# Stick-breaking attention in units of 512 queries, with the gain of its norm applied where the transposed result is evicted

## The chip, the core and the metric

The kernel runs on one core of a Trainium2 chip. The metric is the device time of the whole program in microseconds: the median of several executions. One execution is also profiled; its rows are read below. The core has a matmul engine (PE, with its weight loads shown apart as PEld), a vector engine (DVE), a scalar engine for activations (ACT), GpSimd (POOL) and SyncE (SP), which here issues all transfers.

## What is computed

One decoder layer over 2048 positions and width 1024, in float32. Only the part that the change touches is shown: stick-breaking attention of 8 heads of 64, then an RMS norm over the 64 values of a head with the gain `sb_norm`.

```python
def one_block(args):
    q_blk, t0 = args
    rel = (t0 + jnp.arange(Q_BLOCK))[:, None] - k_pos[None, :]
    strict = rel > 0
    z = jnp.einsum('bhqd,bhkd->bhqk', q_blk, k) * scale
    log_beta = jax.nn.log_sigmoid(z)
    log_1mb = jnp.where(strict, jax.nn.log_sigmoid(-z), 0.0)
    between = lax.cumsum(log_1mb, axis=3, reverse=True) - log_1mb
    a = jnp.where(strict, jnp.exp(log_beta + between), 0.0)
    return jnp.einsum('bhqk,bhkd->bhqd', a, v)
...
sb_o = _rmsnorm(_stick_breaking_attention(sq, sk, sv), sb_norm[l])
mix = jnp.concatenate([diff_o, sb_o], axis=-1) @ w_o[l]
x = x + _rmsnorm(mix, attn_post_norm[l])
```

Before it stand a norm of the input and one q/k/v projection; beside it 4 heads of differential attention with 128 values; after it the output projection and a conv-gated FFN.

## The kernel before

The program is written as a stream of operations for a planner. `op` (L165) records an operation with its engine, an estimated duration, what it depends on and the buffers it uses; `Plan.run` (L180) then simulates the engines with these estimates and fixes the order of the instructions on each engine: of the operations that are ready, and whose buffers are free, the one that was recorded earliest in the planner's own time (`plan.now`) goes first. `copy` (L464) and `split` (L455) can go to either of two engines. So the estimates (`c_mm`, `c_act`, `c_scan`, L43 to L67) shape the order, and the hardware then runs each engine's list in order with semaphores. Buffers are tags with a count (`T`, L337): three PSUM banks "z" for scores, two "t" for transposes, one "o" for results, two "g" for projections; two each of `thi` and `tlo`; one each of `ot`, `os`, `sq`, `mix`, `mo`; and two rings, "w" of 8192 and "a" of 4096 columns, which are taken and given back in order of making.

Precision comes from splitting float32 values into a high and a low part (`hi`, `lo`), so most products are made of two or three matmuls.

Work is staged as follows. Heads come in 8 groups g: 0 to 3 are one differential head each, 4 to 7 are two stick-breaking heads m each. A projection pass p makes q, k and v of some groups for a range of 256-position tiles, and stores them to DRAM. `merge` (L928) interleaves the steps of heads and of projection passes in proportion to their estimated cost, so that the PE has projection matmuls among the attention's. At the end (L1379 to L1389) the last passes are merged with the last heads, the steps up to the mark (7, 5) run alone, and the remaining heads are merged with the first 8 blocks of the output projection (`wo_block`, L1086). `ffn_all` (L1178) follows.

In `sb_stream` (L954) a unit is (n, m, c): n stands for a group g and 256 queries s, m for a head, c for 512 keys, from the diagonal chunk down to 0. `front` (L959) makes, for each of two blocks jj of 128 queries, the scores z (L702, and L705 adds the mask on a diagonal), two sigmoids on ACT (L969 into a row `gm` of ring "a", L971 into a row `be` of ring "w"), a reversed running product on DVE (`scan`, L977), which starts from the last value of the chunk before (its row stays live as the carry), and a product on POOL (L982). A memset on POOL (L967) sets the last column of `gm`. Two units later `tstep` (L1012) transposes two key blocks by two query blocks into one "t" bank (`transp`, L712; L720), evicts it as `thi` (ACT or DVE, L466 and L467) and `tlo` (DVE, L734), and the step after multiplies with v (L1000): 256 queries wide, once with `thi` and once with `tlo`. On a diagonal the evictions are in two pieces, 256 and 128 wide.

`fin_sb` (L793) ends (g, s) for both heads together: copy the result out of "o" (L466), transpose (L799), add the two halves of v (L804, DVE), square (L806, POOL), sum (L807, DVE), mean and power -1/2 (L382 DVE, L384 POOL), then four scalar_tensor_tensor of 64 columns that multiply by the norm and by `sbn`, the gain broadcast to all partitions (L816, DVE). `mix_out` (L758) transposes the 256 columns back (L763), copies them out of PSUM (L466 or L467) and stores them to DRAM. `prefetch` (L746) loads q one s ahead and k, v one chunk ahead.

## Time and profile before

| | |
|---|---|
| median of the runs (3) | 3089.27 us |
| lowest and highest | 3088.21 and 3093.78 us |
| the profiled execution | 3094.23 us, of which the span 3092.5 us |
| mean granted clock of the PE | 0.992 |
| PE busy | 2984.5 us (97%), 17352 matmuls |
| DVE busy | 2252.0 us (73%) |
| ACT busy | 1442.9 us (47%) |
| POOL busy | 951.6 us (31%) |
| chain that ended last | PE 48% of the span, nearly all in the FFN (L1226 30%, L1311 16%) |

The profile is of one execution. A busy time is the time in which an engine had at least one instruction under way; matmuls overlap, so a busy PE isn't a PE at its peak. Times in the rows are in us from the start of the span, durations of one instruction in ns. An "idle before" is the time that the engine stood idle ahead of the instructions of a group, with what released it. Names of tiles stand without their numbers; ring_w and ring_a are the rings.

### The profile page before, as it was taken

Reading aid. Unit: us, or ns where it says so; the run is one execution under the profiler, and the core shown is the slowest. Engines: PE = TensorE matmul, PEld = TensorE weight load, DVE = VectorE, ACT = ScalarE, POOL = GpSimd, SP = SyncE. Lnnn points to the kernel's source line nnn. Section 1 sums busy time; section 2 is a strip of 40 time slices with the busy share of each in tenths; the row PEclk is TensorE's granted clock in tenths of the full one; section 3 lists DMA queues with packets and bytes.
Section 4 is the critical chain, followed back from the end, with each engine's and each line's share of the span. In section 5 each row is a group of like instructions: output and inputs, shape, how many; then the busy total and the mean of one; then the engine's idle time right before and its main releaser. Section 6 shows DMA issues by size and latency. Waiting matters only on the chain. (4 is left out here: it accounts for less than half of the span.)

```text
span 3092.5 us, 48117 instructions
## 1 busy us (share of the span) xinstructions
PE 2984.5 (97%) x17352; PEld 2610.4 (84%) x17352; DVE 2252.0 (73%) x4327; ACT 1442.9 (47%) x2913; POOL 951.6 (31%) x1047
## 2 busy tenths in 40 slices
PE   7999999999999999889999999999999999999998
PEld 7899999999888888868877888888888888888887
DVE  4658878897999999998754864387744776277742
ACT  4434545555777767666643433233322433233321
POOL 1001002002766777675411211033301332023310
PEclk9999999999999999999999999999999999999999
DMA  8776656655634366533363333443344333343332
GB/s 264 246 209 186 185 151 201 171 156 159 188 122 130 95 194 185 151 100 112 110 214 126 102 100 116 121 134 96 96 129 143 96 99 106 119 141 101 96 123 82
DMA packets 392146, 437.11 MB, mean 141 GB/s; under 512 B 20096, under 2 KB 328164, under 8 KB 381668
## 3 DMA queue, kind: packets, MB, share of 16 engines
q1 hardware_dynamic: 391908, 434.05, 46.7%
q8 instruction: 136, 2.23, 0.3%
q14 instruction: 102, 0.84, 0.1%
HBM read 333.30 MB, written 100.67 MB: 140 GB/s over the span
## 5 line engine op out<-in xcount | busy, mean ns | idle before, releaser
L1226 PE MATMUL pu<-fh,fhi 128*128 128x512 f32 x2816 | 869.0, 390 | 0.2 <-ACT fu L1234 0.2
L1226 PEld LDWEIGHTS pu<-fh,fhi 128*128 128x128 f32 x2816 | 529.4, 188 | 110.5 <-ACT fu L1234 0.6
L461 DVE TENSOR_TENSOR flo<-fraw,fhi 128x1024 fp32r<-128x1024 f32 x186 | 233.0, 1254 | 488.6 <-ACT fhi L458 488.5
L1226 PE MATMUL pu<-fh,flo 128*128 128x512 f32 x1408 | 549.2, 390 | 0.0
L982 POOL TENSOR_TENSOR ring_w<-ring_w,ring_a 128x512 f32<-128x512 f32 (+2 forms) x320 | 387.9, 1224 | 220.3 <-DVE ring_a L977 121.1
L605 PE MATMUL g<-hT,big 128*128 128x256 f32 x3072 | 447.8, 288 | 7.3 <-DVE st L638 4.3
L458 ACT CAST fhi<-fraw 128x1024 fp32r<-128x1024 f32 x253 | 265.5, 1051 | 397.4 <-PE py L1311 218.6
L1311 PE MATMUL py<-fhi,gt 128*128 128x512 f32 x1408 | 435.9, 390 | 0.0
L605 PEld LDWEIGHTS g<-hT,big 128*128 128x128 f32 x3072 | 405.4, 192 | 19.8 <-DVE st L638 4.4
L977 DVE TENSOR_TENSOR_SCAN ring_a<-ring_a 128x513 f32<-128x513 f32 (+2 forms) x320 | 412.8, 1316 | 6.1 <-ACT ring_a L969 6.1
L702 PE MATMUL z<-k,q 128*128 128x512 f32 (+3 forms) x1280 | 362.5, 376 | 10.4 <-ACT ring_a L969 7.0
L466 ACT CAST thi<-t 128x512 fp32r<-128x512 f32 (+2 forms) x472 | 221.6, 492 | 210.1 <-PE t L720 179.3
L1311 PEld LDWEIGHTS py<-fhi,gt 128*128 128x128 f32 x1408 | 264.5, 188 | 60.0
L1226 PEld LDWEIGHTS pu<-fh,flo 128*128 128x128 f32 x1408 | 264.7, 188 | 54.9
L734 DVE TENSOR_TENSOR tlo<-t,thi 128x512 fp32r<-128x512 f32 (+2 forms) x528 | 281.6, 556 | 34.6 <-ACT thi L466 28.4
L459 POOL TENSOR_TENSOR flo<-fraw,fhi 128x1024 fp32r<-128x1024 f32 x78 | 195.8, 2510 | 338.9 <-DVE fhi L457 171.2
L1311 PE MATMUL py<-flo,gt 128*128 128x512 f32 x704 | 277.8, 395 | 0.0
L720 PE MATMUL t<-ident,ring_w 128*128 128x128 f32 x1632 | 253.2, 276 | 22.4 <-DVE tlo L734 18.5
L1250 POOL TENSOR_TENSOR gt<-fy,gt 128x512 fp32r<-128x512 f32 x88 | 118.4, 1347 | 493.9 <-ACT gt L1249 483.0
L1239 DVE SCALAR_TENSOR_TENSOR fy<-fu,cw,fy 128x512 f32<-128x512 f32 x176 | 239.6, 1361 | 6.2
L384 POOL TENSOR_TENSOR sm<-sm,neghalf 128x2 f32<-128x2 f32 (+1 forms) x72 | 76.8, 1067 | 536.5 <-DVE sm L382 534.7
L602 PE MATMUL g<-big,hT 128*128 128x256 f32 x1536 | 227.4, 288 | 6.3 <-DVE st L624 1.5
(158 smaller groups left out, 4697.4 us busy)
## 6 DMA issues: line engine op xcount, KB each, us to landing
fraw<-in_w_up_dram SPq DMA_DIRECT2D x176, 512.0 KB, 3.8
hT<-hd SPq DMA_DIRECT2D x64, 1024.0 KB, 7.0
fraw<-in_w_down_dram SPq DMA_DIRECT2D x88, 512.0 KB, 3.8
q<-qd SPq DMA_DIRECT2D x128, 256.0 KB, 4.3
hd<-hT SPq DMA_DIRECT2D x16, 1024.0 KB, 5.4
qd<-st SPq DMA_DIRECT2D x128, 128.0 KB, 2.6
kd<-st SPq DMA_DIRECT2D x128, 128.0 KB, 2.6
vd<-st SPq DMA_DIRECT2D x64, 256.0 KB, 5.2
```

The source lines that it names most:

```text
L458: "ACT", c_act(n) + 42, lambda: nc.scalar.copy(hi(), raw()))
L461: "DVE", c_dvs(n), lambda: nc.vector.tensor_tensor(lo(), raw(), f32(hi()), ALU.subtract))
L602: nc.tensor.matmul(ps.t[:, cs], hk[:, b, c * P:(c + 1) * P], wv[:, a, k, :], start=first, stop=last)
L605: nc.tensor.matmul(ps.t[:, cs], wv[:, a, k, c * P:(c + 1) * P], hk[:, b, :], start=first, stop=last)
L702: nc.tensor.matmul(ps.t[:, 0:w], q.t[:, m, l, jj * P:(jj + 1) * P], kt.t[:, m, 0:w], start=(l == 0), stop=(l == 1 and not masked))
L720: nc.tensor.transpose(ps.t[:, cc * P:(cc + 1) * P], rows[jj].t[:, (k + kk) * P:(k + kk + 1) * P], ident)
L734: ol = op("DVE", c_dvp(n), lambda sl=sl: nc.vector.tensor_tensor(lo.t[:, sl], ps.t[:, sl], f32(hi.t[:, sl]), ALU.subtract), (oh,), (ps, hi ...
L977: nc.vector.tensor_tensor_scan(gr, gr, gr, 1.0 if cb is None else cb[0].t[:, 0:1], ALU.mult, ALU.bypass)
L982: rdeps.append(op("POOL", c_pool(w), lambda be=be, gm=gm, w=w: nc.gpsimd.tensor_tensor(be.t, be.t, gm.t[:, 1:w + 1], ALU.mult), (o1, o2), ...
L1226: nc.tensor.matmul(ps.t, w3(w)[:, k, :], h.t[:, a, k, :], start=(k == 0 and i == 0), stop=(k == KD - 1 and i == 2))
L1239: nc.vector.scalar_tensor_tensor(y.t, u.t[:, 1:TT + 1], cw[:, 1, f:f + 1], y.t, ALU.mult, ALU.add)
L1311: nc.tensor.matmul(ps.t, gt.t[:, a, j * P:(j + 1) * P], wt.t[:, ms], start=(m == 0 and i == 0), stop=(m == NFT - 1 and i == 2))
```

## The change

Stick-breaking units become (t, g, m, c) with t a tile of 512 queries: four blocks jj in a front, and the transposes follow one unit later, one key block by up to four query blocks in a "t" bank, evicted as one contiguous piece and multiplied with v 512 queries wide. Scores claim the two rows, and transposes claim `thi` and `tlo`, when they are planned. Each head m of 512 queries has its own end (`fin`): the square is made on ACT, the norm is applied to 256 columns in one DVE tensor_tensor with the norms broadcast, and when both heads are done, 512 columns are transposed and evicted by an ACT activation whose scale is `sbn`, now one gain per partition, and stored by two transfers. q is loaded per (t, g, m). The tile `sq` is gone, `mix` and `mo` have 512 columns, `sm` has 20 buffers; in `fin_diff` the square's output goes to spare columns of `ot`. The estimate of a matmul is proportional to its columns. The run up to (7, 5) is gone and the last merges have marks in the new units; (7, 2) is the same place in the work as (7, 4) was. Long stretches of removed lines are cut.

```diff
--- before.py
+++ after.py
@@ -41,7 +41,7 @@
 def c_mm(n):
-    return n / 2.4 + 2 if n > 128 else 80
+    return n * 0.4434
 
@@ -298,7 +298,7 @@
     subln = const.tile([P, P], F32, name="subln")
-    sbn = const.tile([P, 64], F32, name="sbn")
+    sbn = const.tile([P, 1], F32, name="sbn")
     cw = const.tile([P, 4, 2 * NFT], F32, name="cw")
@@ -335,13 +335,13 @@
     for name, n in (("hT", 4), ("big", 3), ("raw", 2), ("st", 2), ("k", 5), ("v", 5), ("q", 2),
-                    ("thi", 2), ("tlo", 2), ("mo", 1), ("ot", 1), ("os", 1), ("sq", 1), ("mix", 1),
+                    ("thi", 2), ("tlo", 2), ("mo", 1), ("ot", 1), ("os", 1), ("mix", 1),
                     ):
...
     T["t"] = Tag(2, fifo=False, bank=True)
-    T["sm"] = Tag(24, fifo=False)
+    T["sm"] = Tag(20, fifo=False)
     T["w"] = Ring(8 * 1024)
@@ -361,9 +361,9 @@
     sp = pool(left, "sp", "left")
-    fill_tags(sp, {"thi": ([P, 512], F32R), "tlo": ([P, 512], F32R), "mo": ([P, 256], F32),
-                   "ot": ([P, 512], F32), "os": ([P, 256], F32), "sq": ([P, 256], F32),
-                   "mix": ([P, 256], F32), "sm": ([P, 8], F32)})
+    fill_tags(sp, {"thi": ([P, 512], F32R), "tlo": ([P, 512], F32R), "mo": ([P, 512], F32),
+                   "ot": ([P, 512], F32), "os": ([P, 256], F32),
+                   "mix": ([P, 512], F32), "sm": ([P, 8], F32)})
     pp = pool(left, "pp", "left", PSUM)
@@ -444,7 +444,8 @@
                           (o,))
-        mem["sbn"] = load(lambda: sbn, sb_norm[0:1, :].to_broadcast([P, 64]), 32768)
+        mem["sbn"] = [load(lambda m=m: sbn[m * 64:(m + 1) * 64], sb_norm.rearrange("o p -> p o"), 256)
+                      for m in range(2)]
 
@@ -747,6 +748,8 @@
             load_q(*seq[n + 1])
+        else:
+            mem["sb_first"]()
         if s % 2 == 0:
@@ -762,11 +765,11 @@
         o = op("PE", 214, tr, deps, (ps, mx), what="mixT")
-        o = copy(lambda: mo.t, lambda: ps.t[:, 0:256], 256, (o,), (ps, mo))
-        mixs[g, s] = op(SPE, 0, lambda: nc.sync.dma_start(mixd[s][:, g, :], mo.t), (o,), (mo,), 0, 1 << 17, "mstore")
+        o = copy(lambda: mo.t[:, 0:256], lambda: ps.t[:, 0:256], 256, (o,), (ps, mo))
+        mixs[g, s] = op(SPE, 0, lambda: nc.sync.dma_start(mixd[s][:, g, :], mo.t[:, 0:256]), (o,), (mo,), 0, 1 << 17, "mstore")
 
     def fin_diff(g, s, po, last, rinv, rdeps):
-        ot, pq, os_, ss, junk, cm, mx = buf("ot"), buf("t"), buf("os"), small(), buf("sq"), small(), buf("mix")
+        ot, pq, os_, ss, cm, mx = buf("ot"), buf("t"), buf("os"), small(), small(), buf("mix")
         o = copy(lambda: ot.t[:, 0:256], lambda: po.t[:, 0:256], 256, (last,), (po, ot))
@@ -777,9 +780,9 @@
             for jj in range(2):
-                nc.scalar.activation(junk.t[:, 0:P], os_.t[:, jj * P:(jj + 1) * P], AF.Square,
+                nc.scalar.activation(ot.t[:, 256:384], os_.t[:, jj * P:(jj + 1) * P], AF.Square,
                                      scale=rinv.t[:, jj:jj + 1], accum_out=ss.t[:, jj:jj + 1])
-        o = op("ACT", 780, sq, (oc, *rdeps), (os_, junk, rinv, ss))
+        o = op("ACT", 780, sq, (oc, *rdeps), (os_, ot, rinv, ss))
         r, o = rs_ops(lambda: ss.t[:, 0:2], P, 2, (o,), (ss,))
@@ -788,34 +791,6 @@
         o = op("DVE", 71 + 2 * 263 + 127, fin, (o, mem["subln"]), (r, rinv, cm, os_, mx))
-        mix_out(g, s, mx, (o,))
...
         mix_out(g, s, mx, (o,))
@@ -951,86 +926,151 @@
 
-    def sb_stream(seq, begin, lag):
...
+    def sb_stream():
+        units = [(t, g, m, c) for g in range(4, 8) for t in range(NTT) for m in range(2) for c in range(t, -1, -1)]
+        qts, live, carry, pos, mxs = {}, {}, {}, {}, {}
+        chain_ = {"av": None, "t": None}
         pend = deque()
 
-        def tstep(n, m, c, k):
-            rows, rdeps, nb, _ = live[n, m, c]
-            live[n, m, c, k] = transp(rows, rdeps, k, nb, chain["t"])
-            chain["t"] = live[n, m, c, k][4]
+        def loads(u):
+            t, g, m, c = units[u]
+            if c != t:
+                return
+            q = buf("q")
+            assert qstore[g, 2 * t] and qstore[g, 2 * t + 1]
+            qf = lambda: q.t.rearrange("p a b n -> p (a b n)").rearrange("p (l s) -> p l s", l=2)
+            qts[t, g, m] = qf, q, [load(
+                lambda r=r: f32(qf()[r * 64:(r + 1) * 64]), qd[g][:, m, :, t * TT:(t + 1) * TT], 1 << 18, (q,),
+                [*qstore[g, 2 * t], *qstore[g, 2 * t + 1]], what="qload") for r in range(2)]
+            if (g, c) not in kv:
+                load_kv(g, c)
+
+        mem["sb_first"] = lambda: (loads(0), loads(1))
+
+        def front(u, jj):
+            t, g, m, c = units[u]
+            diag = c == t
+            w = (jj + 1) * P if diag else 512
+            (qf, q, ql), (kt, _, kl, _) = qts[t, g, m], kv[g, c]
+            be, gm, ps = buf("w", w), buf("a", w + 8), buf("z")
+
+            def z():
+                for l in range(2):
+                    nc.tensor.matmul(ps.t[:, 0:w], qf()[:, l, jj * P:(jj + 1) * P], kt.t[:, m, 0:w],
+                                     start=(l == 0), stop=(l == 1 and not diag))
+                if diag:
+                    nc.tensor.matmul(ps.t[:, w - P:w], identr, masks, start=False, stop=True)
+            o0 = op("POOL", 40, lambda: nc.gpsimd.memset(gm.t[:, w:w + 1], 1.0), (), (gm,))
+            o = op("PE", 2 * c_mm(w) + (60 if diag else 0), z, [*ql, kl, mem["masks"]], (ps, q, kt, be, gm), what="z")
+            o1 = op("ACT", c_act(w), lambda: nc.scalar.activation(
+                gm.t[:, 0:w], ps.t[:, 0:w], AF.Sigmoid, scale=-1.0), (o,), (gm, ps), what="sig")
+            o2 = op("ACT", c_act(w), lambda: nc.scalar.activation(
+                be.t[:, 0:w], ps.t[:, 0:w], AF.Sigmoid), (o,), (be, ps), what="sig")
+            cb = None if diag else carry[jj]
+
+            def scan():
+                gr = gm.t[:, 0:w + 1][:, ::-1]
+                nc.vector.tensor_tensor_scan(gr, gr, gr, 1.0 if cb is None else cb[0].t[:, 0:1], ALU.mult, ALU.bypass)
+            o1 = op("DVE", c_scan(w), scan, [o0, o1] + ([cb[1]] if cb else []), [gm] + ([cb[0]] if cb else []),
+                    what="scan")
+            carry[jj] = gm, o1
+            o = op("POOL", c_pool(w), lambda: nc.gpsimd.tensor_tensor(
+                be.t[:, 0:w], be.t[:, 0:w], gm.t[:, 1:w + 1], ALU.mult), (o1, o2), (be, gm), what="mul")
+            live.setdefault(u, []).append((be, o))
+
+        def tstep(u, kb):
+            t, g, m, c = units[u]
+            j0 = kb if c == t else 0
+            ps, hi, lo = buf("t"), buf("thi"), buf("tlo")
+            rows = live[u]
+
+            def tr():
+                for jj in range(j0, 4):
+                    nc.tensor.transpose(ps.t[:, jj * P:(jj + 1) * P], rows[jj][0].t[:, kb * P:(kb + 1) * P], ident)
+            o = op("PE", 109 * (4 - j0), tr, [rows[jj][1] for jj in range(j0, 4)] + (
+                [chain_["t"]] if chain_["t"] else []), [*(rows[jj][0] for jj in range(j0, 4)), ps, hi, lo], what="T")
+            chain_["t"] = o
+            sl = slice(j0 * P, 512)
+            n = 512 - j0 * P
+            oh = copy(lambda: hi.t[:, sl], lambda: ps.t[:, sl], n, (o,), (ps, hi), "hi")
+            ol = op("DVE", c_dvp(n), lambda: nc.vector.tensor_tensor(
+                lo.t[:, sl], ps.t[:, sl], f32(hi.t[:, sl]), ALU.subtract), (oh,), (ps, hi, lo), what="lo")
             if pend:
                 av(*pend.popleft())
-            pend.append((n, m, c, k))
-
-        for u in range(len(units) + lag):
+            pend.append((u, kb, hi, lo, oh, ol, sl))
+
+        def av(u, kb, hi, lo, oh, ol, sl):
+            t, g, m, c = units[u]
+            if (t, g, m) not in pos:
+                pos[t, g, m] = buf("o")
+            po = pos[t, g, m]
+            _, v, _, vl = kv[g, c]
+            n = sl.stop - sl.start
+            last = c == 0 and kb == 3
+
+            def go(src, is_lo):
+                nc.tensor.matmul(po.t[:, sl], v.t[:, kb, m * P:(m + 1) * P], src.t[:, sl], start=c == t and kb == 0 and not is_lo,
+                                 stop=is_lo and last)
+            o = op("PE", c_mm(n), lambda: go(hi, False), [oh, *vl] + ([chain_["av"]] if chain_["av"] else []),
+                   (po, hi, v), what="av")
+            chain_["av"] = op("PE", c_mm(n), lambda: go(lo, True), [ol, o], (po, lo, v), what="av")
+            if last:
+                fin(t, g, m, po, chain_["av"])
+
+        def fin(t, g, m, po, last):
+            ot, pq, os_, ss = buf("ot"), buf("t"), buf("os"), small()
+            if m == 0:
+                mxs[t, g] = buf("mix"), []
+            mx, done = mxs[t, g]
+            o = copy(lambda: ot.t, lambda: po.t, 512, (last,), (po, ot))
+
+            def tr():
+                for j in range(4):
+                    nc.tensor.transpose(pq.t[:, j * P:(j + 1) * P], ot.t[:, j * P:(j + 1) * P], ident)
+            o = op("PE", 436, tr, (o,), (ot, pq, os_), what="finT")
+            p4 = lambda: pq.t.rearrange("p (c l d) -> p c l d", c=4, l=2)
+            o4 = lambda: os_.t.rearrange("p (c d) -> p c d", c=4)
+            o = copy(o4, lambda: p4()[:, :, 1, :], 256, (o,), (pq, os_))
+            o = op("DVE", c_dvp(256), lambda: nc.vector.tensor_tensor(o4(), p4()[:, :, 0, :], o4(), ALU.add), (o,),
+                   (pq, os_))
+            o1 = op("ACT", c_act(256), lambda: nc.scalar.activation(ot.t[:, 0:256], os_.t, AF.Square), (o,), (os_, ot))
+            o1 = op("DVE", 335, lambda: nc.vector.reduce_sum(
+                ss.t[:, 0:4], ot.t[:, 0:256].rearrange("p (c d) -> p c d", c=4), axis=AX.X), (o1,), (ot, ss))
+            r, o1 = rs_ops(lambda: ss.t[:, 0:4], 64, 4, (o1,), (ss,))
+            done.append(op("DVE", c_dvs(256), lambda: nc.vector.tensor_tensor(
+                mx.t.rearrange("p (j c) -> p j c", j=4)[:, :, m * 64:(m + 1) * 64], o4(), r.t[:, 0:4].unsqueeze(2).to_broadcast([P, 4, 64]), ALU.mult),
+                (o1,), (r, os_, mx)))
+            if m == 0:
+                return
+            ps, mo = buf("t"), buf("mo")
+
+            def mtr():
+                for j in range(4):
+                    nc.tensor.transpose(ps.t[:, j * P:(j + 1) * P], mx.t[:, j * P:(j + 1) * P], ident)
+            o = op("PE", 436, mtr, done, (ps, mx, mo), what="mixT")
+            o1 = op("ACT", c_act(512) + 95, lambda: nc.scalar.activation(
+                mo.t, ps.t, AF.Identity, scale=sbn[:, 0:1]), (o, *mem["sbn"]), (ps, mo))
+            for s in (2 * t, 2 * t + 1):
+                mixs[g, s] = op(SPE, 0, lambda s=s: nc.sync.dma_start(
+                    mixd[s][:, g, :], mo.t[:, s % 2 * 256:(s % 2 + 1) * 256]), (o1,), (mo,), 0, 1 << 17, "mstore")
+
+        for u in range(len(units) + 1):
             if u < len(units):
-                n, m, c = units[u]
...
+                t, g, m, c = units[u]
+                if m == 0 and c == t:
+                    yield (g, t), None
+                    if t < 3:
+                        yield 0.0, lambda g=g, t=t: load_kv(g, t + 1)
+                    elif g < 7:
+                        yield 0.0, lambda g=g: load_kv(g + 1, 0)
+                if u + 2 < len(units):
+                    yield 0.0, lambda u=u: loads(u + 2)
+                for jj in range(4):
+                    yield 2 * c_mm(512), lambda u=u, jj=jj: front(u, jj)
+            if u:
+                for kb in range(4):
+                    yield 436 + 2 * c_mm(512), lambda u=u, kb=kb: tstep(u - 1, kb)
+        yield 0.0, lambda: av(*pend.popleft())
 
@@ -1353,7 +1393,7 @@
 
-    seq = [(g, s) for g in range(8) for s in range(8)]
+    seq = [(g, s) for g in range(4) for s in range(8)]
     setup_parts = [setup_lam, setup_bias, setup_rest, setup_ffn]
@@ -1371,19 +1411,20 @@
 
-    heads = chain(diff_stream(seq, 32), sb_stream(seq, 32, 2))
+    sb = sb_stream()
+    first = next(sb)
+    heads = chain(diff_stream(seq, 32), [first], sb)
     run(qkv_steps(0, 0, 2))
...
                             ((1, 4), 1, 0, 3), ((2, 0), 1, 3, 6), ((2, 4), 1, 6, 8),
-                            ((3, 4), 2, 0, 3), ((4, 0), 2, 3, 6), ((4, 4), 2, 6, 8),
-                            ((5, 4), 3, 0, 3), ((6, 0), 3, 3, 6), ((6, 4), 3, 6, 8),
-                            ((6, 6), 4, 0, 2), ((7, 0), 4, 2, 4), ((7, 2), 4, 4, 6), ((7, 4), 4, 6, 8)):
+                            ((3, 4), 2, 0, 3), ((4, 0), 2, 3, 6), ((4, 2), 2, 6, 8),
+                            ((5, 2), 3, 0, 3), ((6, 0), 3, 3, 6), ((6, 2), 3, 6, 8),
+                            ((6, 3), 4, 0, 2), ((7, 0), 4, 2, 4), ((7, 1), 4, 4, 6), ((7, 2), 4, 6, 8)):
         run(merge(until(heads, *mark), qkv_steps(p, i0, i1)))
     wo_weights()
-    run(until(heads, 7, 5))
     run(merge(until(heads), chain.from_iterable(wo_block(b) for b in range(8))))
```

## Rows read from the trace of the kernel before

**Rows 1.** Busy time by stage: stretch, length, PE, PEld, DVE, ACT, POOL (instructions), clock, DMA share, GB/s

```profile
300.00:400.00 100.00, 99.84 (x775) 96.02 (x775) 86.58 (x314) 52.42 (x126) 7.10 (x7) 1.00 0.63 176
...
790.00:1340.00 550.00, 503.97 (x3748) 462.41 (x3748) 536.98 (x776) 400.00 (x911) 398.07 (x559) 0.99 0.50 148
1340.00:1515.00 175.00, 161.90 (x901) 136.01 (x900) 153.41 (x218) 112.08 (x271) 105.78 (x144) 0.96 0.33 104
```

**Rows 2.** Groups of PE instructions, 790 to 1340 us: count | busy us, mean ns | idle before

```profile
L720 PE MATMUL t<-ident,ring_w 128*128 128x128 f32 x852 | 132.8, 276 | 14.6 <-DVE tlo L734 12.7 <-DVE sm L382 0.5 <-DVE os L804 0.4
L605 PE MATMUL g<-hT,big 128*128 128x256 f32 x810 | 121.3, 288 | 0.7 <-DVE st L638 0.7
L702 PE MATMUL z<-k,q 128*128 128x512 f32 x354 | 111.6, 407 | 3.7 <-ACT ring_a L969 3.5
L1000 PE MATMUL o<-tlo,v 128*128 128x256 f32 x398 | 98.0, 317 | 3.8 <-DVE tlo L734 3.3
L1000 PE MATMUL o<-thi,v 128*128 128x256 f32 x398 | 95.5, 311 | 1.7 <-ACT thi L466 1.0 <-ACT big L458 0.4 <-DVE ot L467 0.2
L602 PE MATMUL g<-big,hT 128*128 128x256 f32 x432 | 63.7, 285 | 1.5 <-DVE st L624 1.5
```

**Rows 3.** The chain that ended last, in order of time: start us, us, what

```profile
1589.51 0.87 PE t L1139 x8
...
1717.24 163.51 PE pu L1226 x720
```

**Rows 4.** Timeline of the PE, near 1205 us: start us, us, engine, line, operation

```profile
1205.53 3.04 PE L605 MATMUL g<-hT,big 128*128 128x256 f32 x24
```

**Rows 5.** Groups of DVE instructions, 790 to 1340 us

```profile
L977 DVE TENSOR_TENSOR_SCAN ring_a<-ring_a 128x513 f32<-128x513 f32 x173 | 254.1, 1487 | 0.6 <-ACT ring_a L969 0.6
L734 DVE TENSOR_TENSOR tlo<-t,thi 128x512 fp32r<-128x512 f32 x174 | 113.5, 670 | 3.9 <-ACT thi L466 2.7 <-PE o L1000 1.2
L816 DVE SCALAR_TENSOR_TENSOR mix<-os,sm,sbn 128x64 f32<-128x64 f32 x97 | 43.0, 500 | 2.7 <-POOL ring_a L967 1.8 <-POOL sm L384 0.8
...
L734 DVE TENSOR_TENSOR tlo<-t,thi 128x256 fp32r<-128x256 f32 x50 | 20.3, 406 | 0.5 <-ACT thi L466 0.5
...
L734 DVE TENSOR_TENSOR tlo<-t,thi 128x128 fp32r<-128x128 f32 x50 | 13.8, 277 | 0.0
...
L804 DVE TENSOR_TENSOR os<-t,os 128x256 f32<-128x256 f32 x25 | 10.0, 401 | 0.2
```

**Rows 6.** Timeline of all engines, 1000 to 1018 us: DVE's scans and POOL's products

```profile
1011.10 1.09 POOL L982 TENSOR_TENSOR ring_w<-ring_w,ring_a 128x512 f32<-128x512 f32 x1 [1.49 <-DVE ring_a L977]
...
1014.63 1.27 DVE L977 TENSOR_TENSOR_SCAN ring_a<-ring_a 128x513 f32<-128x513 f32 x1
...
1016.40 1.47 DVE L977 TENSOR_TENSOR_SCAN ring_a<-ring_a 128x513 f32<-128x513 f32 x1
...
1016.79 1.98 POOL L982 TENSOR_TENSOR ring_w<-ring_w,ring_a 128x512 f32<-128x512 f32 x1
```

**Rows 7.** Groups of POOL instructions, 790 to 1340 us

```profile
L806 POOL TENSOR_TENSOR sq<-os 128x256 f32<-128x256 f32 x25 | 27.0, 1081 | 1.0 <-DVE os L804 0.9
```

**Rows 8.** Groups of instructions over the whole span, ACT and DVE

```profile
L780 ACT ACTIVATE sq<-os,sm 128x128 f32<-128x128 f32 x64 | 25.7, 401 | 2.8 <-DVE os L467 1.2
...
L461 DVE TENSOR_TENSOR mt<-mr,mt 128x256 fp32r<-128x256 f32 x30 | 15.6, 520 | 21.8 <-ACT mt L458 20.7 <-PE t L720 0.5
...
L969 ACT ACT_TABLE_LOAD x1 | 1.3, 1283 | 0.0
```

**Rows 9.** Waits of ACT, 790 to 1340 us: us in total, times, longest

```profile
ACT ring_a L969 <- DVE ring_a L977: 23.2, 36, 2.4
```

**Rows 10.** Waits of the PE, 1290 to 1520 us

```profile
PE t L720 <- DVE tlo L734: 9.4, 6, 2.7
```

**Rows 11.** Timeline of the PE, the first matmuls of the output projection

```profile
1363.85 1.68 PE L1101 MATMUL g<-big,mt 128*128 128x512 f32 x6
```

**Rows 12.** Timeline of ACT, a Square of the output projection near 1403 us

```profile
1403.04 0.59 ACT L1117 ACTIVATE r<-g 128x512 f32<-128x512 f32 x1
```

87 lines of the change are left out of this document (1 added, 86 removed).

## Prediction

> **What bounds the kernel now.** I read the stages first, then the groups inside the stage that changes, then single instructions. The table of stages [rows 1] splits the span by what runs. Up to about 790 us the projection and the differential heads run, and a window there has the PE at 99.8%. From 790 to 1340 us stick-breaking heads run beside the last projection passes: DVE is busy 537.0 of 550 us (97.6%), the PE 504.0. From 1340 to 1515 us the last stick-breaking units run beside the output projection: PE 161.9 and DVE 153.4 of 175. After it the output projection ends and the FFN follows, PE-bound: the FFN's matmuls of 512 columns come every 163.51/720 = 0.227 us [rows 3] and nothing in the change alters their number.
>
> In the middle stage PE's busy time hides slack, for matmuls overlap. Counted by their spacing, 0.227 us for 512 columns, 0.87/8 = 0.109 us for a transpose [rows 3] and about 0.12 us for 256 columns (24 in 3.04 us, less the drain of the last) [rows 4], the PE needs there [rows 2] 852 x 0.109 = 93, (810 + 432) x 0.12 = 149, 354 x 0.227 = 80 and (398 + 398) x 0.12 = 95 us, 417 together, and some 48 for the narrower forms: 465 of 550 us, 85%. So DVE sets the pace in this stage and the PE has about 85 us of room.
>
> The Trainium skill (Trainium Kernel Development and Optimization, Performance Expectations) says that matmul busy time is a bad measure of nearness to the limit and points to the weight loads' busy share. The trace agrees: weight loads are busy 462.4 of 550 us here and 96.0 of 100 in the window of the differential heads [rows 1]. By busy time alone the room would be 46 us and the PE-bound rival below would be likelier.
>
> **The change, part by part.** The same chunks of scores, sigmoids, scans, products and 128 x 128 transposes are made as before; their widths don't change. What changes:
>
> (a) The end of a head pair, 32 times in all, 25 of them in the middle stage. Four DVE scalar_tensor_tensor on 64 elements (97 records, 43.0 us, 500 ns each [rows 5]) become one tensor_tensor on 256. No row has that operand pattern. Its nearest are 128x256 tensor_tensors with one PSUM input, 401 ns [rows 5], and with both inputs in SBUF, 520 ns [rows 8]; both new inputs are in SBUF, but the 520 holds waits, so I take 0.45 us: 25 x 0.45 = 11. Saved on DVE: 43 - 11 = 32 us, between 30 and 33.
>
> (b) The hi/lo pieces of a diagonal. Before, every 256 queries left a 256-wide and a 128-wide piece: 50 + 50 records, 20.3 + 13.8 = 34.1 us [rows 5]. After, every 512 queries leave pieces of 384, 256 and 128: 25 x (0.54 + 0.41 + 0.28) = 31 us, the 0.54 halfway between the rows for 256 and 512. Saved: 3 us. ACT's casts shrink likewise.
>
> (c) The square of the norm moves from POOL (25 in the stage, 27.0 us [rows 7]) to ACT, a 256-wide activation; the nearest row is a 128-wide Square with a scale, 401 ns [rows 8], and twice the width costs between once and twice that; I take 0.5 us x 25 = 12 us on ACT. ACT is busy 400 of 550 us [rows 1], so I cost this at nothing; the cover is the scans DVE does meanwhile, and if they aren't there the chain is no longer than with POOL's 1.08 us. POOL's load also slows DVE: a scan takes 1.27 us beside an idle POOL and 1.47 beside a product, which itself goes from 1.09 to 1.98 us [rows 6]. 27 us of POOL less gives DVE about 27/1.98 x 0.2 = 3 us, between 0 and 5.
>
> (d) sb_norm moves into ACT's eviction of the transposed result: 16 evictions of 512 in place of 32 copies of 256, of which DVE did a few: DVE 2 us less, ACT about even. Stores are the same bytes and number.
>
> (e) The attention-value matmuls: 256 columns become 512, half as many. By spacing two of 256 take 0.24 us and one of 512 0.227, so the PE gains about 400 x 0.013 = 5 us, with bounds of 0 and 15, on an engine that isn't the bound.
>
> (f) The order. The planner's cost of a matmul is now 0.4434 ns a column, near the measured 0.227 us for 512. The score matmul now claims its two row buffers when it is planned, and a transpose claims thi and tlo. Four scans instead of two must stay live as carries in the ring "a", which holds seven 520-wide rows, so scores can lead the scans by three, not five. That wait is there already: ACT waits 23.2 us in the stage for a scan to free ring "a" [rows 9]. Behind a waiting sigmoid on ACT stand the casts that the PE's attention-value matmuls need, and behind a late scan on DVE the lo parts. Freed slot to next scan is score, sigmoid and hand-over, some 0.45 + 0.6 + 1 us; three scans and lo parts last 3 x 2.1 us (1.49 + 0.67 [rows 5]). So it should mostly fit; bounds are 0 and 5% of the stage, 27 us, and I take 4 us.
>
> (g) The run of (7,4) alone is gone: the output projection is merged from (7,2) on, which is the same place in the work. Before, the PE's transposes waited thereabouts for DVE, 9.4 us in 6 waits [rows 10], and the first output matmul came at 1363.85 us [rows 11]. Its operands must be loaded first in either kernel, so of these 9 us I count 4, between 0 and 9. In the stage of 175 us DVE saves 40 x 7/25 = 11 us more, but the PE is busy there for all but 13 us: 2 us.
>
> DMAs: query loads are 2 per (g, t, m) against 2 per (g, s), equal in number and bytes, and moved past nothing on SP's queue but stores that it already carries. The norm's gain is loaded by two small transfers before it is needed.
>
> **Sum.** DVE in the middle stage: 32 + 3 + 3 + 2 = 40 us of 537. At the same share of busy time the stage would fall from 550 to 509 us, where the PE needs 465 - 5 = 460, or 90%. With less room on the PE some saving comes back as PE waits; I count 0.85 of it, 34 us, less 4 for (f), plus 6 for (g): 36 us. The profiled execution, 3092.5 us of span and 3094.2 in all, would become 3058; the median of the runs stands 5 us below it, which makes 3053.
>
> **Rivals.**
> 1. All of it and more: the planner keeps DVE at 97.6% and its 40 us come in full, (c) gives 2 more, (g) 9 and the last stage 7 of DVE's 11: 58 us, 3031. For it: DVE is the sole bound by the counts. Against: the PE's need of 90%.
> 2. The PE or the ring takes over: if the PE can't be kept at more than 87% of its need, with its groups waiting on other engines' rows, the stage lasts 460/0.87 = 529 us and 21 are gained; if (f) costs its 27 us, 40 - 27 + 6 = 19. About 3070 to 3075. For it: the PE's transposes and the sigmoids wait for DVE already [rows 9, 10]. Against: elsewhere the same PE runs at 99.8% busy [rows 1].
> 3. Slower: the claim of thi and tlo at the transpose closes a loop: transposes 4 x 0.109 and a drain of 0.17 (276 ns of one [rows 2] less 0.109), a cast like the 512-wide activation of 0.59 [rows 12], lo 0.67, attention-value 2 x 0.227 and a drain of 0.18, then the next but one. That is 2.5 us without queues; two steps of DVE work take 2 x 2.1 = 4.2. If each pass also waits for a scan (1.49), a sigmoid (0.6) and a group of projection matmuls (6 x 0.12), it is 5.3, so 2.65 a step instead of 2.1: 174 full steps x 0.55 = 96 us lost against 40 saved, 3145. It decides from 4.2 us on; half of those waits gives 3.9, under the bound, so I give it little; a milder form, 4.6 us, loses 35 us and gains 40, no change.
> 4. The norm's Square needs another activation table than Sigmoid: a load takes 1283 ns [rows 8], two each for 32 ends, 82 us on ACT with 150 us to spare in the stage, for the loss of about the gain: 3089 to 3110. The run before has one load at the sigmoids' line [rows 8], although the output projection's Squares run in the stage that sigmoids last through, one at 1403.04 us [rows 12]: so 2%. The Trainium skill (ScalarE: Activation LUTs, Table sets) names copy and identity as members of every set, not Square; the trace's single load speaks against it.
> The change may also fail to save: if the new tensor_tensor took 4 x 500 ns, (a) would vanish and the gain be 8 us.
>
> **How the numbers follow.** Forecast case, 3040 to 3066: 0.52. Rival 1: 0.16. Rival 2 and a costly (a): 0.14. No change, by a milder rival 3: 0.06. Slower, by rivals 3 and 4 and an order that the planner lays badly: 0.12. A measurement here tells apart about 0.2%, 6 us, so faster means under 3083: 0.80; same 0.08; slower 0.12. The range takes rivals 1 and 2 and leaves out most of 3 and 4: 3024 to 3082.
>
> **What would show it.** DVE stays at 96% or more from 790 us on, and stick-breaking ends 35 to 45 us earlier, the FFN's rows unchanged. The new tensor_tensor has 32 records of 0.4 to 0.5 us, attention-value matmuls number 640, no further table load appears. Wrong would be: DVE at 92% or less with transposes waiting for lo (rival 3), ACT waiting for ring "a" far over 23 us (f), or PE busy without gaps in the stage (rival 2).

## The result, and the profile after

The changed kernel takes 3117.28 us (median of 4 runs, 3113.78 to 3119.09) against 3088.93 of the kernel before beside it: a ratio of 1.0087, 95% interval 1.0070 to 1.0105. By the medians it is 28 us slower, by the ratio 27; 36 us faster was predicted. Ratios below are all to runs of the kernel before on the same chip in the same hour, and 0.001 is 3.1 us; kernels that didn't run beside each other are compared by ratio. One execution of e3 below took 14289.68 us where its eight others took 3096.19 to 3099.84, and it is left out of its median and its ratio. The profiled execution has a span of 3115.6 us, 23.1 more than before.

The stages first, the same stretches as in [rows 1] (length, then PE, PEld, DVE, ACT, POOL with their instructions, clock, DMA share, GB/s):

```profile
790.00:1340.00 550.00, 496.28 (x3251) 434.72 (x3251) 516.93 (x669) 379.68 (x852) 379.43 (x521) 0.97 0.48 147
1340.00:1515.00 175.00, 160.46 (x846) 129.63 (x845) 155.01 (x220) 112.10 (x270) 94.95 (x134) 0.99 0.34 107
```

In the middle stage DVE, the bound, is busy 516.9 us where it was 537.0: 94.0% instead of 97.6%. ACT lost as much, the PE 8 us. Nothing took the place of DVE as the busiest engine; all of them wait. The waits of that stretch (engine, tile, line, what it waited for: us in total, times, longest) say on what:

```profile
PE o L1012 <- DVE tlo L996: 28.4, 36, 2.9
PE t L1049 <- DVE tlo L996: 7.8, 5, 2.5
PE t L989 <- DVE os L1034: 5.8, 9, 1.1
...
DVE tlo L996 <- ACT thi L467: 22.5, 24, 1.9
DVE thi L468 <- PE t L989: 4.0, 6, 1.3
...
ACT thi L467 <- PE t L989: 101.1, 92, 4.2
```

Read from the bottom it is a ring: ACT waits for the PE's transposes to make `thi`, DVE waits for `thi` to make `tlo`, and the PE's attention-value matmuls (L1012) wait for `tlo`. In the kernel before two of the three were short and the third half as long, and ACT waited 23.2 us for ring "a" [rows 9], a wait that is down to 1.6 us:

```profile
PE o L1000 <- DVE tlo L734: 3.6, 7, 1.5
...
DVE tlo L734 <- ACT thi L466: 3.2, 5, 1.6
...
ACT thi L466 <- PE t L720: 50.9, 68, 2.9
```

The granted clock of the PE fell too, from 0.99 to 0.97 over the stage. The lower of its two levels (1.2 GHz) comes right behind stretches in which the PE stood: from 1206.80 to 1210.20 us it is busy 1.77 of 3.40 us, and the granted clock is 0.80 there and 0.70 in the next 3.40 us, in which it is busy throughout.

The groups of the same stretch after, PE and DVE (count | busy us, mean ns | idle before, with what ended it):

```profile
L989 PE MATMUL t<-ident,ring_w 128*128 128x128 f32 x806 | 133.1, 282 | 7.1 <-DVE os L1034 5.8 <-DVE tlo L996 1.3
L1012 PE MATMUL o<-tlo,v 128*128 128x512 f32 x167 | 75.5, 452 | 22.0 <-DVE tlo L996 21.5
...
L973 DVE TENSOR_TENSOR_SCAN ring_a<-ring_a 128x513 f32<-128x513 f32 x173 | 257.9, 1504 | 2.8 <-ACT ring_a L965 2.3 <-POOL ring_w L977 0.2
L996 DVE TENSOR_TENSOR tlo<-t,thi 128x512 fp32r<-128x512 f32 x167 | 111.0, 670 | 22.3 <-ACT thi L467 22.1
L1040 DVE TENSOR_TENSOR mix<-os,sm 128x256 f32<-128x256 f32 x22 | 19.0, 866 | 1.5 <-POOL sm L384 0.8 <-POOL ring_a L963 0.7
L382 DVE TENSOR_SCALAR sm<-sm 128x4 f32<-128x4 f32 x22 | 13.8, 626 | 0.0
L996 DVE TENSOR_TENSOR tlo<-t,thi 128x384 fp32r<-128x384 f32 x23 | 12.4, 540 | 0.0
```

The transposes done by 1340 us are 806 where they were 852 [rows 2]; at 852 in 550 us, the 46 missing are 30 us of the stage. The new tensor_tensor (L1040) takes 866 ns, not the 450 of step (a).

The second loss lies where nothing was changed. In the chain that ended last (start us, us, what) the down projection of a tile of the FFN reads after, and below it before:

```profile
2018.94 239.41 PE pu L1266 x1056
2258.35 123.20 PE py L1351 x528
```

```profile
2002.97 239.36 PE pu L1226 x1056
2242.33 120.86 PE py L1311 x528
```

The same 528 matmuls in the same order take 2.35 us more, 233.3 instead of 228.9 ns each, in each of four tiles: 9.4 us. The up projection (L1266) is unchanged within 0.05 us.

### The profile page after: what moved, and what is told of

The parts are those of the page before. It is cut to its first block, busy times and chain, and to the rows that moved or that the text cites. A ratio compares the mean times of both kernels' runs of the same rounds, so it can differ in the third digit from the quotient of the medians.

```text
span 3115.6 us, 46750 instructions
## 1 busy us (share of the span) xinstructions
PE 2999.2 (96%) x16840; PEld 2586.1 (83%) x16840; DVE 2231.4 (72%) x4230; ACT 1437.6 (46%) x2873; POOL 932.5 (30%) x1008
## 5 line engine op out<-in xcount | busy, mean ns | idle before, releaser
L1266 PE MATMUL pu<-fh,fhi 128*128 128x512 f32 x2816 | 868.2, 389 | 0.0
L1266 PEld LDWEIGHTS pu<-fh,fhi 128*128 128x128 f32 x2816 | 528.9, 188 | 110.4
L1266 PE MATMUL pu<-fh,flo 128*128 128x512 f32 x1408 | 548.2, 389 | 0.0
L977 POOL TENSOR_TENSOR ring_w<-ring_w,ring_a 128x512 f32<-128x512 f32 (+2 forms) x320 | 411.6, 1297 | 238.1 <-DVE ring_a L973 127.6
L606 PEld LDWEIGHTS g<-hT,big 128*128 128x128 f32 x3072 | 412.2, 192 | 22.7 <-DVE st L625 5.6
L467 ACT CAST thi<-t 128x512 fp32r<-128x512 f32 (+3 forms) x422 | 215.5, 518 | 255.3 <-PE t L989 127.1
L1266 PEld LDWEIGHTS pu<-fh,flo 128*128 128x128 f32 x1408 | 264.4, 188 | 55.4
L460 POOL TENSOR_TENSOR flo<-fraw,fhi 128x1024 fp32r<-128x1024 f32 x74 | 186.0, 2514 | 356.8 <-ACT fhi L459 201.2
L603 PEld LDWEIGHTS g<-big,hT 128*128 128x128 f32 x1536 | 210.1, 195 | 11.1 <-POOL big L460 2.0
L996 DVE TENSOR_TENSOR tlo<-t,thi 128x512 fp32r<-128x512 f32 (+1 forms) x320 | 188.1, 593 | 31.0 <-ACT thi L467 30.5
L965 ACT ACTIVATE ring_a<-z 128x512 f32<-128x512 f32 (+2 forms) x320 | 178.0, 557 | 30.1 <-PE z L959 15.7
```

The source lines that it names most:

```text
L460: o2 = op("POOL", c_pool(n), lambda: nc.gpsimd.tensor_tensor(lo(), raw(), f32(hi()), ALU.subtract), (o1,), bufs, lead, what="split").alt(" ...
L467: return op("ACT", c_act(n), lambda: nc.scalar.copy(dst(), src()), deps, bufs, what=what).alt("DVE", c_dvp(n), lambda: nc.vector.tensor_co ...
L603: nc.tensor.matmul(ps.t[:, cs], hk[:, b, c * P:(c + 1) * P], wv[:, a, k, :], start=first, stop=last)
L606: nc.tensor.matmul(ps.t[:, cs], wv[:, a, k, c * P:(c + 1) * P], hk[:, b, :], start=first, stop=last)
L977: o = op("POOL", c_pool(w), lambda: nc.gpsimd.tensor_tensor(be.t[:, 0:w], be.t[:, 0:w], gm.t[:, 1:w + 1], ALU.mult), (o1, o2), (be, gm), w ...
L996: ol = op("DVE", c_dvp(n), lambda: nc.vector.tensor_tensor(lo.t[:, sl], ps.t[:, sl], f32(hi.t[:, sl]), ALU.subtract), (oh,), (ps, hi, lo), ...
```

## Experiments

The loss thus has two places, and the gain that was forecast is missing besides. The theory that I tested was the prediction's rival 3 in a milder form (the claim of `thi` and `tlo` at the transpose) with an address effect in the FFN; the main rivals were the new estimate of a matmul, which reorders everything, and the new end itself.

**The narrow column (e1).** The only thing that the FFN could notice is where its tiles lie: `sbn` went from 64 columns to one, so the FFN's tiles on that side start 224 bytes lower (these starts are the allocator's, in steps of 32 bytes; the expectation below says 252). Not every tile gets its old place back in e1: the rings lie behind `mo` and `mix`, which are wider than before.

In the changed kernel:

```diff
-    sbn = const.tile([P, 1], F32, name="sbn")
+    sbn = const.tile([P, 64], F32, name="sbn")
```

Only column 0 is used.

> The changed kernel with one edit: the tile of the norm's gain is given 64 columns again, of which one is used, so that every tile allocated after it keeps the address it had before the change (the changed kernel moves them by 252 bytes). Address theory: the down projection's matmuls of the FFN, which came every 0.2289 us before and 0.2333 us after with the same sequence (528 in 120.85 against 123.20 us), go back to 0.229, four times 2.35 us, so the kernel takes about 3108 us; addresses may also be behind some of the longer GpSimd products (1468 against 1360 ns), then a few us more. Order theory alone: the down projection stays at 0.2333 and the time at 3117 us.

Measured: 3104.96 us, 1.0047 (1.0032 to 1.0062), 12 us less. The down projection is back:

```profile
2252.93 120.86 PE py L1351 x528
```

The middle stage stays as in the changed kernel, DVE 517.09 of 550 us. So some 12 us of the 28 are an effect of addresses, 9.4 of them in the down projection; the rest is within the interval, and no row shows where it lies.

**The estimate of a matmul, alone (e2).**

In the kernel before:

```diff
-    return n / 2.4 + 2 if n > 128 else 80
+    return n * 0.4434
```

> The kernel before with one edit: the planner's cost of a matmul is 0.4434 ns a column. If the new cost is behind the worse order, this kernel takes 3100 us or more; if the order comes from the new units and claims, it stays within 5 us of 3089. If the cost is behind the slower down projection, its 528 matmuls take 123.2 us here; by the address theory 120.9.

Measured: 3094.54 us, 1.0016 (1.0007 to 1.0026): 5.7 us lost, although 0.4434 ns a column gives the 0.227 us that 512 columns take [rows 3]. That is between its two forecasts. I take it that the order is a matter of all estimates together (argued, not shown); by itself this one is no main cause.

**The claim at the transpose (e3).**

In `tstep` of the changed kernel:

```diff
-                [...], [*(rows[jj][0] for jj in range(j0, 4)), ps, hi, lo], what="T")
+                [...], [*(rows[jj][0] for jj in range(j0, 4)), ps], what="T")
```

> The changed kernel with one edit: a transpose no longer claims thi and tlo when it is planned; they are claimed by the eviction, as in the kernel before. Loop theory (a transpose must wait until the attention-value matmuls two steps earlier have given the buffers back, so the PE stands before them waiting for lo, 25.4 us in 31 waits from 790 to 1303 us, and DVE then waits for the cast, 22.5 us): both waits fall to 5 us or so and the kernel takes 3095 to 3105 us. If the units of 512 themselves or ring a are behind it, it stays at 3112 to 3120.

Measured: 3097.94 us, 1.0025 (1.0015 to 1.0036): 19 us less. Stage and waits, 790 to 1340 us:

```profile
790.00:1340.00 550.00, 500.07 (x3360) 438.53 (x3359) 538.73 (x708) 398.29 (x886) 375.37 (x538) 0.99 0.50 152
...
PE o L1012 <- DVE tlo L996: 6.3, 12, 1.0
DVE tlo L996 <- ACT thi L467: 2.2, 4, 1.2
ACT thi L467 <- PE t L989: 59.6, 63, 2.9
ACT ring_a L965 <- DVE ring_a L973: 7.8, 9, 2.1
```

DVE is back at 98.0%, and the ring of waits is open: 28.4 us became 6.3, 22.5 became 2.2, 101.1 became 59.6. With the claim, the planner may put a transpose on the PE only once the attention-value matmuls that free one of the two pairs are done in its simulation, so the PE's fixed order has them ahead of it; on the chip those wait for `tlo`, and the transposes, the scores and the projection matmuls stand behind them. The granted clock of the stage is 0.99 again; how much of the 19 us is the clock and how much the waits themselves, no run separates.

**The end of a head pair, alone (e4).** The kernel before in its units of 256, with the square on ACT, one tensor_tensor for the norm and `sbn` in ACT's eviction:

```diff
-        o = op("POOL", c_pool(256), lambda: nc.gpsimd.tensor_tensor(sq.t, os_.t, os_.t, ALU.mult), (o,), (os_, sq))
+        o = op("ACT", c_act(256), lambda: nc.scalar.activation(sq.t, os_.t, AF.Square), (o,), (os_, sq))
...
-                    nc.vector.scalar_tensor_tensor(m4[:, jj, m, :], o4()[:, c, :], r.t[:, c:c + 1], sbn,
-                                                   ALU.mult, ALU.mult)
+            nc.vector.tensor_tensor(
+                mx.t.rearrange("p (j m d) -> p m j d", j=2, m=2), os_.t.rearrange("p (m j d) -> p m j d", j=2, m=2),
+                r.t[:, 0:4].rearrange("p (m j) -> p m j", m=2).unsqueeze(3).to_broadcast([P, 2, 2, 64]), ALU.mult)
...
-        o = copy(lambda: mo.t, lambda: ps.t[:, 0:256], 256, (o,), (ps, mo))
+            o = op("ACT", c_act(256) + 95, lambda: nc.scalar.activation(
+                mo.t, ps.t[:, 0:256], AF.Identity, scale=sbn[:, 0:1]), (o, *mem["sbn"]), (ps, mo))
```

> The kernel before, in units of 256 queries and with its order of claims, with the new end of a head pair alone: the square on ACT, the norm applied by one DVE tensor_tensor on 256 columns, the gain applied by ACT's eviction; the tile of the gain keeps 64 columns. If DVE sets the pace of the stage from 790 to 1340 us, the DVE time saved (four of 0.49 us against one of 0.45 to 0.85, 32 times) shows as 25 to 40 us less, 3050 to 3065. If the pace is set by the loop between the engines and DVE's busy time only fills it, the gain is under 8 us, 3081 or more.

Measured: 3075.35 us, 0.9952 (0.9937 to 0.9968): 13.5 us faster, between the two forecasts, so neither is borne out as it was put. The good part of the change is here, but smaller than steps (a), (c) and (d) made it. The DVE groups of 790 to 1340 us:

```profile
L979 DVE TENSOR_TENSOR_SCAN ring_a<-ring_a 128x513 f32<-128x513 f32 x179 | 269.0, 1522 | 0.7 <-ACT ring_a L971 0.7
...
L817 DVE TENSOR_TENSOR mix<-os,sm 128x256 f32<-128x256 f32 x26 | 23.8, 914 | 2.6 <-POOL sm L384 1.8 <-POOL ring_a L969 0.8
```

The 26 tensor_tensors take 23.8 us and not 11.7, and a scan 1522 ns where it took 1487 [rows 5], which is 6 us over 179 scans. Of the 43.0 us of the old instructions [rows 5] less than half comes back.

**Two and three causes together (e5, e6).** e5 has the column padded and the claim late; e6 the old estimate besides.

> The changed kernel with two parts undone: the column of sb_norm's gain lies in a tile of 64 columns, so that everything behind it in SBUF starts where it did before, and a transpose no longer claims thi and tlo. Theory (two costs that have nothing to do with each other, 12 and 19 us): 3117 - 12 - 19 = 3086, the down projection back at 120.9 us for 528 matmuls, DVE busy 499 of 510 us between 790 and 1300. Rival (both act through the same order, so that the second undoing finds nothing left): 3097.

> The same, and the planner's cost of a matmul is that of the kernel before (n / 2.4 + 2, 80 for narrow ones). Theory (the new estimate costs some 6 us by itself, as the kernel before lost 5.7 by it): 3080. Rival (the new estimate suits the units of 512 and was fitted to them): 3086 or more.

Measured: 3087.10 us, 0.9989 (0.9980 to 0.9999), and 3078.94 us, 0.9961 (0.9948 to 0.9974). By the ratios the costs add up: 12, 18 and 9 us. With the three undone the changed kernel is 11 us faster than the one before.

**The address, from the other side (e7).**

In the kernel before:

```diff
     sbn = const.tile([P, 64], F32, name="sbn")
+    gap = const.tile([P, 1], F32, name="gap")
```

> The kernel before with one unused column of 4 bytes a partition behind the tile of sb_norm's gain, nothing else. Theory (where the operands start in SBUF sets how fast matmuls of the down projection follow each other): the 528 matmuls take 123.2 us instead of 120.9 in each of 4 tiles, 3098 to 3101. Rival (the slower down projection needs another thing of the change, such as the order of the weight loads): 3089 as before.

Measured: 3100.38 us, 1.0033 (1.0022 to 1.0044). One unused column slows the kernel before by 10.5 us:

```profile
2238.43 123.20 PE py L1312 x528
```

**The run alone (e8).**

In the kernel before:

```diff
-    run(until(heads, 7, 5))
```

> The kernel before without the run up to (7, 5) alone: the output projection is merged with the heads from (7, 4) on. Theory by the prediction's step (g): 4 us less, 3085, between 0 and 9. Rival (the first output matmul waits for its operands at about 1360 us in either order, and blocks of the output projection that come too early hold back the heads): 3089 to 3095.

Measured: 3085.98 us, 0.9985 (0.9975 to 0.9994): 3.9 us. Step (g), 4 us, holds.

**Which address (e9, e15, e18).** A matmul of the down projection reads two operands: rows of the weights, on the left side, and a block of `gt`, on the right. Three kernels move one or the other. All are the changed kernel with some unused columns. e9 (gt 32 bytes lower) and, with 56 in place of 8, e18 (224 bytes lower):

```diff
         fill_tags(gp, {"gt": ([P, 2, TT], F32R)})
+        gap = gp.tile([P, 8], F32, name="gap")
```

e15 (the weights 32 bytes higher):

```diff
     sbn = const.tile([P, 1], F32, name="sbn")
+    gap = const.tile([P, 8], F32, name="gap")
```

> The changed kernel with 32 unused bytes a partition above the FFN's gt tiles, which lie in another pool than the FFN's weights: gt moves down by 32 bytes, nothing else moves. In the kernel before, gt and the weights both start 32 bytes past a multiple of 64; in the changed one gt still does, and the weights start on a multiple; here both start on a multiple. Theory (what counts is how the starts of a matmul's two operands lie to each other): the 528 matmuls of the down projection fall back from 123.2 to 120.9 us in each of 4 tiles, 3117 - 9 = 3108. Rival (what counts is where the moving operand, the weights, starts by itself): 123.2 as in the changed kernel, 3117.

> The changed kernel with 32 unused bytes a partition behind the gain's column: the FFN's weights start at 64864 (32 past a multiple of 64, as before the change, though 192 bytes lower) and gt at 139232. So far: weights 65056 with gt 139232 gave 120.9 us for 528 matmuls, 64832 with 139232 gave 123.2, 64832 with 139200 gave 122.7. Theory (the moving rows' start counts by itself, 32 past a multiple of 64 is the fast place): 120.9, 3105 to 3108. Rival (the distance of the two operands counts: here it is the same modulo 256 as in the run that gave 122.7): 122.7, 3113.

> The changed kernel with 224 unused bytes a partition above the gt tiles: the FFN's weights stay at 64832, as in the changed kernel, and gt moves to 139008, so that their distance is 74176 bytes as in the kernel before. Distances so far: 74176 gave 120.9 us for the 528 matmuls, 74368 (twice, at two different starts) 122.7, 74400 and 74144 123.2. Theory (the distance alone decides): 120.9 in each of 4 tiles, 3117 - 9 = 3108. Rival (the starts by themselves count too, and a start 32 past a multiple of 64 is needed): 122 to 123.2, 3113 to 3117.

Measured: e9 3113.19 us, 1.0069 (1.0052 to 1.0085); e15 3114.59 us, 1.0078 (1.0063 to 1.0093); e18 3106.36 us, 1.0051 (1.0035 to 1.0068). One row of the chain of each:

```profile
2256.29 122.71 PE py L1352 x528
```

```profile
2259.26 122.71 PE py L1352 x528
```

```profile
2253.55 120.85 PE py L1352 x528
```

The table gives where the first tile of each starts, in bytes of a partition, as the allocator places it; the further tiles follow in steps of 4096.

| kernel | weights start | gt starts | distance | 528 matmuls |
|---|---|---|---|---|
| before | 65056 | 139232 | 74176 | 120.85 us |
| e18 | 64832 | 139008 | 74176 | 120.85 us |
| changed | 64832 | 139232 | 74400 | 123.20 us |
| e7 | 65088 | 139232 | 74144 | 123.20 us |
| e9 | 64832 | 139200 | 74368 | 122.71 us |
| e15 | 64864 | 139232 | 74368 | 122.71 us |

e9 spoke against both of its forecasts as they were put (neither 120.9 nor 123.2). e15 fell to its rival, and e18 settled it for these distances: in both pairs of equal distance the time is equal, though the two start elsewhere; 74400 and 74144, which differ by 256, also agree. In the up projection both operands lie on the left side and move together, and its time stays within 239.36 to 239.41 us. Which distances are good besides 74176 wasn't tried.

**The lead of the scores (e10, e11, e13).** All start from e6. The prediction's step (f) said that four live carries leave scores a lead of three rows in ring "a", and that the score now claims its rows.

e10:

```diff
-            o = op("PE", [...], z, [*ql, kl, mem["masks"]], (ps, q, kt, be, gm), what="z")
+            o = op("PE", [...], z, [*ql, kl, mem["masks"]], (ps, q, kt), what="z")
```

e11 (e13 has both):

```diff
-    T["w"] = Ring(8 * 1024)
-    T["a"] = Ring(4 * 1024)
+    T["w"] = Ring(7 * 1024)
+    T["a"] = Ring(5 * 1024)
```

> As the run with the late claim of thi and tlo, the padded column and the old estimate of a matmul (3079), and the score no longer claims its two rows: a score may be planned before its rows in the rings are free, as in the kernel before. Theory (with thi and tlo claimed late and scans as the bound, the claim of the rows only moves the wait from ACT to the planner): within 3 us of 3079, ACT's waits for ring a back at some 20 us. Rival (the claim holds back the PE's scores, which the prediction's step (f) priced): 3070 to 3074.

> As that run too (3079, score claiming its rows), with the ring of running products 5120 columns long instead of 4096, and the ring of the other rows 7168 instead of 8192, so that scores can lead the scans by five rows and not three. Theory by the prediction's step (f), which priced the short lead at 4 us: 3075. Rival (the lead was never short, since DVE is busy 495 of 510 us in the stage): 3079, or above where the shorter other ring holds back.

> Units of 512 with the late claim of thi and tlo, the padded column and the old estimate (3079), and now both the longer ring of running products (3069 by itself) and the score that doesn't claim its rows (3074 by itself). Theory (both undo the same thing, the short lead of the scores): 3068 to 3070. Rival (they add up): 3064. Against the 3067 of the kernel with units of 256 and the same new end it also tells what units of 512 are worth by themselves.

Measured: e10 3073.80 us, 0.9949 (0.9934 to 0.9964); e11 3069.34 us, 0.9935 (0.9920 to 0.9949); e13 3065.77 us, 0.9920 (0.9904 to 0.9937). Against e6 by ratio, the claim costs 4 us, the longer ring brings 8, and both together 13: here the rivals of e10 and e13 came nearer, and e11 went 6 us past its theory. The 4 us are not clear of noise (the intervals of e6 and e10 overlap). The theory of e10 held for the wait, which is back, and missed the time by 2 us:

```profile
ACT ring_a L965 <- DVE ring_a L973: 25.9, 40, 2.6
```

Those are 25.9 us of waits on ACT, an engine with room, where e6 has 3.8, and the kernel is no slower with them, rather some 4 us faster.

**Units of 256 with the parts that gain (e12, e14, e16, e17).** e12 is e4 without the run alone; e14 has the two rings of e11 besides; e16 is e12 with the tensor_tensor of the norm on POOL; e17 is e14 and e16 together.

e16 against e12:

```diff
-            nc.vector.tensor_tensor(
+            nc.gpsimd.tensor_tensor(
                 mx.t.rearrange("p (j m d) -> p m j d", j=2, m=2), os_.t.rearrange("p (m j d) -> p m j d", j=2, m=2),
...
-        o = op("DVE", c_dvs(256), fin, (o,), (r, os_, mx))
+        o = op("POOL", c_pool(256), fin, (o,), (r, os_, mx))
```

> The kernel before with the new end of a head pair (3075 by itself) and without the run up to (7, 5) alone (3086 by itself): units of 256 queries, old estimate of a matmul. Theory (the two gains, some 14 and 4 us, lie in different stretches and add up): 3071. Rival (the new end already fills the gap that the lone run left): 3075.

> The kernel before with the new end of a head pair and without the run alone (3067), and the rings of 5120 and 7168 columns instead of 4096 and 8192. Theory (in units of 256 two carries are live, not four, so that the ring already gives a lead of five; DVE is busy 498 of 510 us): 3065 to 3068. Rival (scores wait for the ring there as well, ACT 15.8 us in the stage): 3059.

> The kernel before with the new end and without the run alone (3067), and the new tensor_tensor of the norm on POOL instead of DVE. Theory (DVE loses 32 x 0.84 us, and what a POOL product costs DVE beside it is some 0.2 to 0.4 us each): 27 - 10 = 17 us less in the DVE-bound stages, 3050. Rival (with both inputs in SBUF it holds DVE up as long from POOL, and the longer end of a head pair holds PE's transposes): 3065 or more.

> The kernel before with the new end of a head pair, its tensor_tensor on POOL, without the run alone, and with rings of 5120 and 7168 columns: the parts that gained, without those that lost. Theory (the rings gave 6 us on the kernel with the tensor_tensor on DVE, POOL gave 10, and DVE still is the bound at 499 of 510 us): 3051. Rival (with less DVE work the PE's own order is next, so the two gains overlap): 3055 to 3058.

Measured: e12 3067.12 us, 0.9927 (0.9912 to 0.9942); e14 3060.83 us, 0.9903 (0.9888 to 0.9918); e16 3057.55 us, 0.9893 (0.9879 to 0.9908); e17 3061.39 us, 0.9903 (0.9888 to 0.9918). The gains of the end and of the run alone add up in e12, which is 4 us faster still than forecast. e14 came out between its theory and its rival: the longer ring brings units of 256 some 7 us too, so it is an improvement of its own and no undoing of the change. e13 and e14 have the same parts in the end, the same estimate and rings, and differ in the units: units of 512 are 5 us slower, not faster. Two more things differ, and no run separates them: where the rings start, and that the changed end still claims `os` at its transpose and `mo` at its last one, earlier than in the kernel before. The loss can be seen on DVE at the end of a head, 790 to 1340 us: 26 tensor_tensors take 25.6 us in e13 and 20.2 in e14, and the 26 small instructions of the mean (L382) 15.8 and 8.1. e16 got 10 us of its 17, and shows where part of the rest went; its DVE and POOL groups, 790 to 1340 us:

```profile
L979 DVE TENSOR_TENSOR_SCAN ring_a<-ring_a 128x513 f32<-128x513 f32 x185 | 282.9, 1549 | 1.0 <-POOL ring_a L969 0.4 <-ACT ring_a L971 0.3 <-issue 0.3
...
L984 POOL TENSOR_TENSOR ring_w<-ring_w,ring_a 128x512 f32<-128x512 f32 x183 | 257.6, 1418 | 93.2 <-DVE ring_a L979 50.4 <-ACT thi L467 12.1 <-ACT ring_w L973 8.4
L817 POOL TENSOR_TENSOR mix<-os,sm 128x256 f32<-128x256 f32 x26 | 23.3, 898 | 1.1
```

The 26 instructions leave DVE, and its scans go from 1527 ns in e12 to 1549, which is 4 us over 185 scans. e17 adds the rings and misses both its forecasts: it is no faster than e14, and by ratio 3 us slower than e16, with intervals that overlap. So the two gains are worth no more together than one alone; what holds e17, no run shows. e16 is the fastest kernel here, 34 us under the one before and 60 under the changed one.

## Why the prediction was wrong

It was wrong in sign: forecast 3053, range 3024 to 3082, measured 3117. By the ratios of e1, e5, e6 and e10, each with one thing more undone, the 27 us are 43 of losses (addresses 12, the claim of `thi` and `tlo` 18, the estimate 9, the score's claim 4) against 16 of gain, where the prediction had 4 of losses and 40 of gain. The last two losses depend on the order of undoing, and the claim of the score alone is not clear of noise.

- **Step (f), the one that failed most.** It gave 4 us to the whole order, with bounds of 0 and 27. Measured: 18 + 9 + 4 = 31. Its working looked only at the length of ring "a" and found that the lead "should mostly fit"; a longer ring is worth some 8 us here (e11) but 7 to units of 256 as well (e14), so that was not the place. The 1 us of hand-over in that working stands on no row. It named the claims of the score and of `thi` and `tlo` and the estimate, and put no price of its own on any of them; only rival 3 priced the second.
- **Rival 3, slower.** The mechanism was named and had the right place, transposes that can't start before an older pair is free. It was dismissed because its loop came to 3.9 us against a bound of 4.2. I take the form of that test to be the mistake (this is argued, not shown): a loop that fits on average still stalls each time one piece comes late, since each engine runs a fixed list in order. Its row is there, though not the one I named: not transposes but attention-value matmuls wait for `tlo` (28.4 us after, 6.3 in e3), and DVE is at 94.0%, not at 92% or less. Its milder form was said to lose 35 us and gain 40; the loss was 18 and the gain 16, and the other losses decided the sign.
- **Step (a), mis-sized.** 0.45 us for the tensor_tensor, measured 0.85 (32 of them 27.0 us over the whole span). The rows taken as nearest have an input in PSUM [rows 5] or lie in another stage [rows 8]; in this one a product of POOL beside it makes it three times as long (shown at the end). [Rows 6] showed such a collision and I charged it to the scans only.
- **Step (c), wrong sign.** POOL's 27 us less were to give DVE 3 us. A scan took 1504 ns after and 1522 in e4, against 1487 [rows 5]; why it grew with less POOL work, no run shows. The square itself on ACT is as estimated (0.43 us, 0.5 taken), hidden as said.
- **Steps (b), (d).** The pieces of a diagonal have the times assumed (384 wide 540 ns against 0.54 us). The eviction by ACT takes 692 ns, 16 times, and no further table load appears: rival 4 is out.
- **The gain of the wider units in (b) and (e)**, 3 us on DVE and 5 on the PE, doesn't show: e13 is 5 us slower than e14.
- **Step (g)** holds where it was tried, in the kernel before: 3.9 us against 4, 2 to 8 by the interval.
- **Not foreseen at all:** a tile made narrower moved the FFN's operands, 12 us. The text said of the FFN that nothing in the change alters the number of its matmuls [rows 3]; their number stayed, their pace didn't.
- **The share of 0.85** by which DVE's saving becomes time: e4 saves 20.9 us of DVE over the span (2252.0 to 2231.1) and 13.5 of time, 0.65.

## What to carry to other kernels

In a kernel whose order is planned from estimates, a claim of a buffer that is made earlier can hold back every engine behind it: price it by experiment with the one line undone, not by whether the loop fits on average. After an edit that changes the size of any long-lived tile, compare the pace of untouched stages row by row; if it moved, pad the tile back before judging the edit. And what an instruction costs on DVE is to be read beside the POOL work that it will run with, not from its fastest rows.
